# A streaming encoder step on one core: down product in groups of four feature blocks with the k-tile outermost, and the feed-forward's first weights taken up in the last residual block

## The chip, the core and the metric

The kernel runs on one core of a Trainium2 chip. A core has five engines, each with an instruction queue of its own that is worked off strictly in order: PE (TensorE, matmuls; PEld are its weight loads), DVE (VectorE), ACT (ScalarE), POOL (GpSimd) and SP (SyncE, which here issues DMA transfers). The metric is the device time of one execution in microseconds, median of several runs; lower is better.

## The reference

One inference step of a one-layer encoder for 1024 prompt tokens and 8 streams of 16 tokens, together T = 1152 tokens of width D = 1024, in float32. Only the third part is touched by the change:

```
x  = x + concat(diff_attention, short_conv) @ w_out       # token mixing
x  = x + cross_attention(x) @ w_xo                        # D x D, residual
hf = rms_norm(x, g_ffn)
u  = causal_dwconv3(hf @ w_up)                            # D -> D_FF = 2816
x  = x + (silu(u) * (hf @ w_gate)) @ w_down               # D_FF -> D
y  = rms_norm(x, g_final)
```

## The kernel before, in words

Activations lie transposed: features on the 128 partitions, tokens along the free axis. Every float32 product is made of three fp32r matmuls: each operand x is split into a high part h (a cast, on ScalarE, line 111) and a low part l = x - h (a subtraction, on VectorE or GpSimd, line 112), and h·h + h·l + l·h is summed in PSUM. So every weight block of 128x512 costs a cast and a subtraction ahead of its matmuls (`wh`, `wl`).

*Residual block with w_xo* (`residual_wino`). Eight output blocks of 128 features, each over three chunks of 384 tokens. `block` fetches and splits the weight (`wunit`), multiplies, and `evac` adds x, stores it, scales it into the halves `xa`, `xb` for the feed-forward, and adds up squares on GpSimd (`acc`). Up to here a planner orders the instructions; from the feed-forward on, the order is the one in which the code is written.

*Up and gate product* (`ffn`). One Strassen-Winograd level: for each slab s of 22 there are seven products P1 to P7 of 24 matmuls with 288 columns, `seq` lists them. Weights come as two raw tiles of 128x1024 per slab (`ffn_load`), and four sums S1 to S4 of their quarters are made on GpSimd (`ffn_sum`). The activation side has B11, B21, B22 (split at the block's end, `pair`) and the differences T1 to T4 (`tsubs` makes them, `tsplit` splits them). Before each product n, `read(n-1)` reads the PSUM sums of the last one, `split(n+3)` splits a weight three products ahead, and `at[n]` holds whatever else is due (norm ratio, convolution, gate). There are four buffers for wh and wl each, so the split for product n+4 must wait until product n is done. The gated result goes to DRAM (`gscr`).

*Down product.* The tokens are three tiles c of 512, 384 and 256 columns (`LAST`), the output eight feature blocks j, the sum over k runs over 22 k-tiles (`NFB`). A step takes one 128x512 piece of weights, split three steps ahead (`wsplit`), and mostly 12 matmuls. The list `steps` gives their order:

- tile 0, j = 0..3: k outermost, one step per k-tile, four feature blocks per step (22 steps);
- all else: one feature block j after the other, six steps of four k-tiles each (the sixth of two).

The operands of a tile (22 split pairs of gscr data) come by `qload` (DMA into one of three buffers S2, S3, S4), `qsplit` and `operands`. For tile 0 one is made per step in the first 22 steps; for tiles 1 and 2 all 22 are made during the last two feature blocks of the tile before, in 12 steps. `evac(c, j)` closes a feature block: VectorE multiplies by the norm ratio and adds the residual `ys` (fetched by `xload`), ScalarE squares and scales, GpSimd adds up the squares (in the last tile mostly VectorE). `norm1` sums over partitions on TensorE, `norm2` makes the reciprocal root and multiplies all eight blocks in one go, six on VectorE and two on GpSimd, and stores them, two of the stores being issued on ScalarE's queue.

The PSUM has four tiles `ch` of two banks each in this part.

Of the kernel before, what the change touches and what calls it, by code (L numbers as in the profile page):

```python
# [51 lines left out]
class Step:  # L52
# [122 lines left out]
    def block(self, src, xh, xl, tag, evac):  # L175

        w = self.wunit(src)
        for c in range(NCH):
# [790 lines left out]
    def residual_wino(self, wsrc, xh, xl, xsrc, dst, gi):  # L969
# [6 lines left out]
        self.Tf = [None] * 4  # L976
        for n in range(KT):
# [20 lines left out]
            self.block(wsrc[j], xh, xl, lambda c: ("mm", "tr")[(c + n) % 2], evac)  # L998
            if n % 2 == 0:
                self.B[k]["B11"] = self.pair("hl", "b", h0)  # L1000
            else:
                b11, b22, b12, b21 = xa[k][:, 0:HT], xa[k][:, HT:T], xb[k][:, 0:HT], xb[k][:, HT:T]
                self.B[k]["B21"] = self.pair("hl", "b", b21)
                self.B[k]["B22"] = self.pair("hl", "b", b22)
# [4 lines left out]
                self.tsubs = [sub(b11, b12, b11), sub(b12, b22, b12), sub(b22, b22, b11), sub(b21, b21, b22)]  # L1009
# [11 lines left out]
    def w2(self, x, view=lambda z: z):  # L1021

        m = x.shape[-1] if len(x.shape) == 2 else 512
        h, l = (self.tile("w2", t, [512], 4, F32R)[:, 0:m] for t in ("wh", "wl"))
        self.split(view(h), view(l), x)
        return h, l

    def w2_raw(self, src):
        raw = self.tile("w2", "raw", [1024], 4)[:, 0:src.shape[-1]]
# [3 lines left out]
    def ffn_load(self, s):  # L1033

        i = 4 * (s // 2) + s % 2
        r0, r1 = (self.w2_raw(self.I["w_ug"][u]) for u in (i, i + 2))
# [10 lines left out]
    def ffn(self):  # L1047
# [8 lines left out]
        first = {**reads, "P3": [("d", 1, 10)], "P6": [("b", 1, 1)], "P5": [("c", 1, 1)], "P7": [("b", 11, 10), ("c", 11, 11)]}  # L1056
        second = {**reads, "P5": [("c", 11, 10)], "P7": [("b", 11, 11)]}
        seq = [(0, "P1"), (0, "P3"), (0, "P2"), (0, "P6"), (0, "P5"), (0, "P7"), (1, "P1"), (0, "P4"),
# [4 lines left out]
        self.W, wp, ch = {}, {}, {}  # L1063
# [24 lines left out]
        def product(n):  # L1088
            s, p = seq[n]
            h, l = wp.pop(n)  # L1090
            b, c = opd[p][1], (s, "d" if (s, p) == (0, "P3") else chain[p])
# [109 lines left out]
        def ratio(t):  # L1201

            def f():
                z = self.tile("tu", "z", [T])
                v, y, r = half(z, 0), half(z, 1), half(self.r, t)
# [5 lines left out]
                nc.scalar.activation(r, y, AF.Square)  # L1211
                nc.vector.scalar_tensor_tensor(out=v, in0=v, scalar=-0.5, in1=r, op0=ALU.mult, op1=ALU.mult)
# [21 lines left out]
        put(4, tsplit("T3", (2, 3), (3,)), self.tsubs[3])  # L1234
# [3 lines left out]
        for i in range(last + 1):  # L1238
# [17 lines left out]
            else:  # L1256
                put(7, ratio(0))
                put(8, ratio(1))
# [398 lines left out]
```

## Time and profile before

| | |
|---|---|
| median of 3 runs | 1733.08 us (1730.76 to 1733.68) |
| the profiled execution: its time, its span | 1735.62 us, 1733.8 us |
| PE busy, share of the span | 1669.3 us, 96% |
| DVE, ACT, POOL busy | 60%, 39%, 24% |
| granted TensorE clock, mean | 0.980 |
| L111 casts of weights, ACT, 128x512 | 607 ns mean |
| L112 low parts of weights, DVE, 128x512 | 702 ns mean |
| L112 low parts of weights, POOL, 128x512 | 1326 ns mean |

A row of a timeline reads: start, duration, engine, line, operation, output <- input, shapes, count, and in brackets the idle time of the engine before it with what ended it. PE's busy share says little by itself, since matmuls are pipelined and a slowed clock also counts as busy; the distance of starts tells the rate. A wait is put down to the instruction that came last.

### The profile page before, as it was taken

The numbers are of one execution on the slowest core, as the hardware profiler recorded it, in microseconds if no ns is written. First come the engines' busy times: TensorE is split into PE (matmuls) and PEld (weight loads), VectorE is DVE, ScalarE is ACT, GpSimd is POOL, SyncE is SP. The second block draws the span as 40 slices with busy tenths as digits, with TensorE's granted clock in tenths as the row PEclk, the third lists the DMA queues.
The fourth block names the chain that finished last, engine by engine and source line by source line (L and its number), as shares of the span: only waits on it lengthen the run. The fifth ranks groups of instructions, "written<-read, shape, count | busy, mean of one in ns | idle before, by whom it ended". The sixth has DMA issues, their size and how long they took to land.

```text
span 1733.8 us, 28155 instructions
## 1 busy us (share of the span) xinstructions
PE 1669.3 (96%) x10930; PEld 1579.6 (91%) x10930; DVE 1045.0 (60%) x1707; ACT 678.1 (39%) x1382; POOL 413.9 (24%) x443
## 2 busy tenths in 40 slices
PE   8999989999999999999989999999999999979887
PEld 7999879989899999989988999999999998869787
DVE  8757545777733343376658766666666664444465
ACT  7222543655513332263335433333333354433443
POOL 3223322111113321101335333233223212120100
PEclk9999999999999999999989999999999999999989
DMA  5756877434264434532431222221222265455553
GB/s 197 252 189 208 283 255 197 152 110 128 92 260 142 133 110 183 182 147 85 136 121 38 78 78 78 78 71 64 74 77 78 77 193 173 147 172 173 160 185 123
DMA packets 111366, 246.09 MB, mean 142 GB/s; under 512 B 18176, under 2 KB 63104, under 8 KB 111232
## 3 DMA queue, kind: packets, MB, share of 16 engines
q1 hardware_dynamic: 110368, 243.11, 43.1%
q8 instruction: 86, 1.41, 0.3%
q10 hardware_dynamic: 864, 1.18, 0.2%
q14 instruction: 48, 0.39, 0.1%
HBM read 186.86 MB, written 57.39 MB: 141 GB/s over the span
## 4 chain that ended last, share of the span: by engine, by line
PE 80%; DVE 6%; DMA 5%; ACT 4%; issue 2%; POOL 1%; SPq 0%; DVEq 0%; ACTq 0%; POOLq 0%
PE ch L1102 27%; PE ch L1381 11%; PE mm L148 8%; PE mm L150 8%; PE mm L149 8%; PE tr L148 3%; PE tr L149 3%; PE tr L150 3%; DMA S<-gscr 2%; PE tr L653 2%; DMA ys<-x 1%; PE sc L614 1%; PE tr L640 1%; ACT wh L111 1%; DVE ys L1364 1%
## 5 line engine op out<-in xcount | busy, mean ns | idle before, releaser
L111 ACT CAST wh<-raw 128x512 fp32r<-128x512 f32 x338 | 201.5, 607 | 346.5 <-PE ch L1102 99.9
L112 DVE TENSOR_TENSOR wl<-raw,wh 128x512 fp32r<-128x512 f32 (+1 forms) x284 | 196.6, 702 | 226.2 <-ACT wh L111 225.3
L1102 PE MATMUL ch<-t,wh 128*128 128x288 f32 x1408 | 284.9, 297 | 3.9 <-DVE xb L1111 3.7
L1102 PEld LDWEIGHTS ch<-t,wh 128*128 128x128 f32 x1408 | 227.5, 189 | 4.6 <-issue 3.9
L1102 PE MATMUL ch<-b,wh 128*128 128x288 f32 x1056 | 216.8, 300 | 5.5 <-ACT wh L111 5.5
L1102 PE MATMUL ch<-t,wl 128*128 128x288 f32 x704 | 208.0, 296 | 0.0
L112 POOL TENSOR_TENSOR wl<-raw,wh 128x512 fp32r<-128x512 f32 x54 | 71.5, 1326 | 450.8 <-ACT wh L111 412.6
L1102 PEld LDWEIGHTS ch<-b,wh 128*128 128x128 f32 x1056 | 172.6, 191 | 6.2 <-ACT wh L111 6.0
L148 PE MATMUL mm<-xh,wh 128*128 128x384 f32 x496 | 169.7, 342 | 0.9 <-DVE t L822 0.9
L150 PE MATMUL mm<-xh,wl 128*128 128x384 f32 x496 | 167.9, 338 | 0.0
L149 PE MATMUL mm<-xl,wh 128*128 128x384 f32 x496 | 167.7, 338 | 0.0
L1102 PE MATMUL ch<-b,wl 128*128 128x288 f32 x528 | 157.4, 298 | 0.5 <-DVE wl L112 0.5
L1381 PE MATMUL ch<-t,wh 128*128 128x512 f32 (+2 forms) x544 | 139.5, 343 | 6.5 <-ACT wh L111 6.3
L1102 PEld LDWEIGHTS ch<-t,wl 128*128 128x128 f32 x704 | 133.5, 190 | 0.0
L1381 PEld LDWEIGHTS ch<-t,wh 128*128 128x128 f32 x544 | 97.0, 192 | 15.4 <-ACT wh L111 7.9
L1381 PE MATMUL ch<-b,wh 128*128 128x256 f32 (+2 forms) x384 | 95.8, 341 | 13.0 <-ACT wh L111 13.0
L1102 PEld LDWEIGHTS ch<-b,wl 128*128 128x128 f32 x528 | 101.1, 191 | 1.0 <-DVE wl L112 1.0
L1381 PE MATMUL ch<-t,wl 128*128 128x512 f32 (+2 forms) x272 | 94.0, 346 | 2.8 <-DVE wl L112 2.5
L148 PEld LDWEIGHTS mm<-xh,wh 128*128 128x128 f32 x496 | 93.3, 188 | 3.7 <-issue 1.6
L149 PEld LDWEIGHTS mm<-xl,wh 128*128 128x128 f32 x496 | 93.4, 188 | 0.4
L150 PEld LDWEIGHTS mm<-xh,wl 128*128 128x128 f32 x496 | 93.4, 188 | 0.1
L1045 POOL TENSOR_TENSOR S<-raw,raw 128x512 f32<-128x512 f32 x44 | 72.1, 1640 | 68.1 <-DVE wl L112 63.6
(374 smaller groups left out, 3730.2 us busy)
## 6 DMA issues: line engine op xcount, KB each, us to landing
raw<-in_w_dn SPq DMA_DIRECT2D x51, 512.0 KB, 4.4
raw<-in_w_ug SPq DMA_DIRECT2D x44, 512.0 KB, 4.5
gscr<-xb SPq DMA_DIRECT2D x22, 576.0 KB, 3.2
kv<-in_kc SPq DMA_DIRECT2D x16, 512.0 KB, 5.6
kv<-in_vc SPq DMA_DIRECT2D x16, 512.0 KB, 6.3
qd<-qscr SPq DMA_DIRECT2D x64, 128.0 KB, 3.8
kv<-in_km SPq DMA_DIRECT2D x16, 512.0 KB, 6.0
kv<-in_vm SPq DMA_DIRECT2D x16, 512.0 KB, 5.6
```

Of the source, the lines that this page charges most:

```text
L111: self.nc.scalar.copy(out=h, in_=x)
L112: (eng or self.nc.vector).tensor_tensor(out=l, in0=x, in1=fl(h), op=ALU.subtract)
L148: self.nc.tensor.matmul(out, lhsT=ah, rhs=bh, start=i == 0, stop=False)
L149: self.nc.tensor.matmul(out, lhsT=ah, rhs=bl, start=False, stop=False)
L150: self.nc.tensor.matmul(out, lhsT=al, rhs=bh, start=False, stop=i == n - 1)
L614: nc.tensor.matmul(sc[:, a:b], lhsT=qd[:, m, hl, (i % 2) * P:(i % 2 + 1) * P], rhs=ks[m][:, a:b], start=hl == 0, stop=hl == 1)
L640: nc.tensor.transpose(tr[:, j * P:(j + 1) * P], a[:, kt * P:(kt + 1) * P], self.ident)
L653: nc.tensor.matmul(av[:, qs], lhsT=at[kt // 4][:, kt % 4, qs], rhs=vt[:, kt], start=kt == 0, stop=kt == n - 1)
L1045: self.nc.gpsimd.tensor_tensor(out=w[o], in0=w[x], in1=w[y], op=op)
L1102: nc.tensor.matmul(o, lhsT=w[:, ks], rhs=y[:, ts], start=start and k == 0 and i == 0, stop=k == 3 and i == 2, skip_group_check=True)
L1364: eng.tensor_tensor(out=ys[c, j], in0=ys[c, j], in1=r, op=ALU.mult)
L1381: nc.tensor.matmul(ch[c, j], lhsT=p[:, w], rhs=y, start=k == 0 and e == 0, stop=k == NFB - 1 and e == 2)
```

## The change

1. In the last residual block, right after its own weight is fetched, the first slab's two raw tiles are loaded and its four sums made (`first`, called by `block` through the new argument `then`). The pool `weights` therefore stays open, and the feed-forward's raw tiles and split weights use its buffers together with a smaller pool `w2`: again four raw tiles and four pairs in all.
2. The first slab's products run in the order P1, P2, P3 and go to three PSUM tiles of their own (chains a, d, e); the splits of the last B21 and B22 come after the first two weight splits; the norm ratio of each half is made in two pieces, `ratio1` and `ratio2`, one place apart.
3. The down product runs with k outermost in groups of four feature blocks for tile 0, tile 1 and the first half of tile 2 (110 steps); only the last four feature blocks of tile 2 keep the old form (24 steps). Weights for the groups come from an array laid out so that a load is one contiguous block.
4. The operands of the next tile are made one per step during the second group of a tile, with six buffers in place of three; their low parts on VectorE only (for tile 0 every third stays on GpSimd).
5. A group's four `evac` stand in the first four steps of the next group, its residual loads in the last four steps of its own. `norm1` comes after step 7, `norm2` at step 9 of the next tile's first group, and the final multiplies (`norm3`) one per step in steps 10 to 17, for tiles 0 and 1 all on VectorE and stored by SP.

The core of the diff:

```diff
+        def first():
+            self.ffn_load(0)
+            for d in range(4):
+                self.ffn_sum(0, d)
...
-            self.block(wsrc[j], xh, xl, lambda c: ("mm", "tr")[(c + n) % 2], evac)
+            self.block(wsrc[j], xh, xl, lambda c: ("mm", "tr")[(c + n) % 2], evac, first if n == KT - 1 else None)
...
-        seq = [(0, "P1"), (0, "P3"), (0, "P2"), (0, "P6"), (0, "P5"), (0, "P7"), (1, "P1"), (0, "P4"),
+        seq = [(0, "P1"), (0, "P2"), (0, "P3"), (0, "P6"), (0, "P5"), (0, "P7"), (1, "P1"), (0, "P4"),
...
-                put(7, ratio(0))
-                put(8, ratio(1))
-                put(9, rho(0, 0), rho(0, 10))
+                put(7, ratio1(0))
+                put(8, ratio2(0), ratio1(1))
+                put(9, rho(0, 0), rho(0, 10), ratio2(1))
...
-        steps = [(0, range(4), (k,)) for k in range(NFB)]
-        steps += [(c, (j,), range(4 * u, min(4 * u + 4, NFB)))
-                  for c in range(len(LAST)) for j in range(0 if c else 4, KT) for u in range(6)]
+        steps = [(c, range(4 * g, 4 * g + 4), (k,)) for c in range(3) for g in range(2) for k in range(NFB) if (c, g) != (2, 1)]
+        NG = len(steps)
+        steps += [(2, (j,), range(4 * u, min(4 * u + 4, NFB))) for j in range(4, KT) for u in range(6)]
...
-            graw[q] = self.tile("ws", ("S2", "S3", "S4")[q % 3], [512])[:, 0:b - a]
+            e = q % 6 if c else q % 3
+            graw[q] = self.tile("ws" if e < 3 else "t8", ("S2", "S3", "S4")[e % 3], [512])[:, 0:b - a]
...
-            self.split(h, l, x, nc.gpsimd if q % 3 == 0 else None)
+            self.split(h, l, x, nc.gpsimd if q < NFB and q % 3 == 0 else None)
...
         for i, (c, js, ks) in enumerate(steps):
+            g, k = js[0] // 4, ks[0]
             wsplit(i + 3)
...
+            if len(js) > 1:
+                if k < 4 and i >= NFB:
+                    evac(*((c, k) if g else (c - 1, 4 + k)))
+                if g == 0 and c and k == 9:
+                    norm2(c - 1)
+                if g == 0 and c and 9 < k < 18:
+                    norm3(c - 1, k - 10)
+                if 18 <= k:
+                    xload(c, 4 * g + k - 18)
+                if g and c < 2:
+                    operands(NFB * (c + 1) + k + 1, 6)
...
+            if len(js) == 1 and js[0] == 4 and ks[0] < 16:
+                evac(c, k // 4)
             step(i)
...
-            j = js[0]
-            if c < 2 and j >= 6:
-                operands(NFB * (c + 1) + (ks[0] // 4 + 1 if j == 6 else min(10 + ks[0], NFB)))
+            if g == 0 and c and len(js) > 1 and k == 7:
+                norm1(c - 1)
```

How the change moves instructions, at three places. First GpSimd at the end of the residual block (`acc` are the sums of squares of the last chunks, `S` and `raw` the first and second slab's weight sums, `t` the low parts of T3 and T4). Before:

```order
L225 TENSOR_TENSOR acc_8210<-acc_8210,sq_9078 128x384
L225 TENSOR_TENSOR acc_8210<-acc_8210,sq_9112 128x384
L225 TENSOR_TENSOR acc_8210<-acc_8210,sq_9145 128x384
L1045 TENSOR_TENSOR S_1661_9178<-raw_9174,raw_9176 128x512
L1045 TENSOR_TENSOR raw_9176<-raw_9176 128x512
L1045 TENSOR_TENSOR S_1662_9181<-raw_9176,raw_9174 128x512
L1045 TENSOR_TENSOR S_1663_9183<-raw_9174,S_1662_9181 128x512
```

The same place in the changed kernel:

```order
L1059 TENSOR_TENSOR S_1648_9052<-raw_9048,raw_9050 128x512
L1059 TENSOR_TENSOR raw_9050<-raw_9050 128x512
L1059 TENSOR_TENSOR S_1649_9055<-raw_9050,raw_9048 128x512
L1059 TENSOR_TENSOR S_1650_9057<-raw_9048,S_1649_9055 128x512
L227 TENSOR_TENSOR acc_8210<-acc_8210,sq_9089 128x384
L227 TENSOR_TENSOR acc_8210<-acc_8210,sq_9123 128x384
L227 TENSOR_TENSOR acc_8210<-acc_8210,sq_9156 128x384
```

The four sums of the first slab moved ahead of the last block's three sums of squares.

Second, VectorE at the same place (`xc` the last evacuated chunk, `b` low parts of B21 and B22 of the last k-tile, `wl` low parts of the first weights). Before:

```order
L988 TENSOR_TENSOR xc_9140<-tr_9115,xc_9140 128x384
L993 SCALAR_TENSOR_TENSOR xa_8922<-xc_9140,c_6_79,c_9_84 128x384
L112 TENSOR_TENSOR b_9153<-xa_8922,b_9152 128x576
L112 TENSOR_TENSOR wl_9190<-raw_9174,wh_9189 128x512
L112 TENSOR_TENSOR wl_9194<-S_1663_9183,wh_9193 128x512
L112 TENSOR_TENSOR wl_9198<-raw_9174,wh_9197 128x512
```

Now:

```order
L998 TENSOR_TENSOR xc_9151<-tr_9126,xc_9151 128x384
L112 TENSOR_TENSOR wl_9185<-raw_9048,wh_9184 128x512
L1003 SCALAR_TENSOR_TENSOR xa_8922<-xc_9151,c_6_79,c_9_84 128x384
L112 TENSOR_TENSOR b_9189<-xb_8923,b_9188 128x576
L112 TENSOR_TENSOR b_9193<-xa_8922,b_9192 128x576
L112 TENSOR_TENSOR wl_9197<-S_1650_9057,wh_9196 128x512
```

P1's low part is no longer here (it stands two chunks earlier), P2's stands right behind the last PSUM read, and the split of B21 now comes after it.

Third, ScalarE at the handover from token tile 0 to tile 1 (`t`, `gx`, `b` are operand casts for tile 1, `wh` weight casts, `sq` and `ys` the square and the scale of an evacuation). Before:

```order
L111 CAST t_15631<-S_2558_15597 128x384
L111 CAST t_15637<-S_2561_15603 128x384
L111 CAST t_15643<-S_2564_15609 128x384
L111 CAST t_15649<-S_2571_15635 128x384
L111 CAST wh_15655<-raw_15437 128x512
L111 CAST gx_15671<-S_2574_15641 128x384
L111 CAST gx_15677<-S_2577_15647 128x384
L111 CAST gx_15683<-S_2580_15653 128x384
L111 CAST gx_15689<-S_2585_15675 128x384
L111 CAST wh_15695<-raw_15437 128x512
```

Now:

```order
L111 CAST b_15653<-S_2547_15513 128x384
L111 CAST wh_15671<-raw_15507 128x512
L111 CAST b_15677<-S_2552_15535 128x384
L111 CAST wh_15695<-raw_15507 128x512
L226 ACTIVATE sq_15704<-ys_15601 128x512
L1366 ACTIVATE ys_15601<-ys_15601,c_6_79 128x512
L111 CAST wh_15722<-raw_15553 128x512
L226 ACTIVATE sq_15729<-ys_15625 128x512
L1366 ACTIVATE ys_15625<-ys_15625,c_6_79 128x512
L111 CAST wh_15745<-raw_15553 128x512
```

Operand casts stood four between two weight casts; now one stands between two, and after the handover a square and a scale stand between every two weight casts, four times over.

More of the change, by code (lines that the diff above doesn't have):

```diff
@@ L173, in finish, with block @@
             self.todo.pop(0)()
-    def block(self, src, xh, xl, tag, evac):
+    def block(self, src, xh, xl, tag, evac, then=None):
         w = self.wunit(src)
+        if then:
+            then()
         for c in range(NCH):
@@ L1018, in pair, with w2, w2_raw @@
         return h, l
[L1021 to L1025, printed above, removed]
+    def w2(self, x):
+        m = x.shape[-1]
+        self.wn += 1
+        h, l = (self.tile("w2" if self.wn % 4 == 2 else "weights", t, [512], 1 if self.wn % 4 == 2 else 3, F32R)[:, 0:m]
+                for t in ("wh", "wl"))
+        self.split(h, l, x)
         return h, l
-    def w2_raw(self, src):
-        raw = self.tile("w2", "raw", [1024], 4)[:, 0:src.shape[-1]]
+    def w2_raw(self, src, odd):
+        raw = self.tile("w2" if odd else "weights", "raw", [1024], 2)[:, 0:src.shape[-1]]
         self.nc.sync.dma_start(out=raw, in_=src)
@@ L1318, in qsplit, with operands @@
             x = graw.pop(q)
-            e = q % 28
-            pool, tag, bufs = ("tb", "t", 24) if e < 12 else ("t8", "gx", 8) if e < 16 else ("hl", "b", 24)
-            h, l = (self.tile(pool, tag, [512 if pool == "t8" else HT], bufs, F32R)[:, 0:x.shape[-1]] for _ in range(2))
-            self.split(h, l, x, nc.gpsimd if q % 3 == 0 else None)
+            pool, tag = ("tb", "t") if q % 24 < 12 else ("hl", "b")
+            h, l = (self.tile(pool, tag, [HT], 24, F32R)[:, 0:x.shape[-1]] for _ in range(2))
+            self.split(h, l, x, nc.gpsimd if q < NFB and q % 3 == 0 else None)
             gx[divmod(q, NFB)] = h, l
-        def operands(upto):
+        def operands(upto, lead=3):
             while done[0] < min(upto, 3 * NFB):
@@ L1353, in norm1 @@
             a, b = LAST[c]
-            ch[c] = self.bank("ch")[:, 0:b - a]
+            ch[c] = ch[c, 4]
             for i, z in enumerate(sq[c]):
@@ L1370, in step @@
             h, l = wp.pop(N + i)
-            for j in js:
+            for e, j in enumerate(js):
                 if (c, j) not in ch:
@@ L1377, in step @@
                 for x, k in enumerate(ks):
-                    w = slice((j if len(js) > 1 else x) * P, (j if len(js) > 1 else x) * P + P)
+                    w = slice((e + x) * P, (e + x + 1) * P)
                     gh, gl = gx[c, k]
-                    for e, (p, y) in enumerate(((h, gh), (h, gl), (l, gh))):
-                        nc.tensor.matmul(ch[c, j], lhsT=p[:, w], rhs=y, start=k == 0 and e == 0, stop=k == NFB - 1 and e == 2)
-        self.ffn_load(0)
-        sums(0, 0, 1, 2, 3)()
+                    for m, (p, y) in enumerate(((h, gh), (h, gl), (l, gh))):
+                        nc.tensor.matmul(ch[c, j], lhsT=p[:, w], rhs=y, start=k == 0 and m == 0, stop=k == NFB - 1 and m == 2)
         new_u(0)()
-        for n in range(3):
-            split(n)
-        for f in self.tsubs[:3]:
+        split(0)
+        split(1)
+        for f in self.tsubs[:2]:
+            f()
+        split(2)
+        for f in self.tsubs[2:5]:
             f()
```

106 lines of the change are left out of this document (52 added, 54 removed).

## The prediction

> **What bounds the kernel now.** I read the stages first, then what TensorE waits for in them, then what stands ahead of those releasers on their own engines. All times are of the one profiled execution: its span is 1733.8 us and its own time 1735.6, that is 1.8 more, and 2.5 above the median of the three runs (1733.1).
>
> The stage table (columns: stage, length, busy us of PE, PEld, DVE, ACT, POOL, granted clock, DMA share, GB/s):
> ```profile
> 892.97:946.20 53.23, 43.05 (x272) 41.03 (x273) 38.62 (x50) 25.87 (x44) 23.38 (x18) 0.89 0.17 54
> 946.20:1405.40 459.20, 459.20 (x3431) 459.20 (x3432) 321.75 (x417) 165.74 (x251) 140.81 (x186) 0.99 0.24 78
> 1519.50:1562.60 43.10, 32.13 (x149) 27.06 (x147) 22.93 (x36) 18.53 (x36) 8.95 (x7) 0.92 0.55 174
> 1618.80:1668.90 50.10, 37.55 (x217) 34.52 (x215) 26.32 (x46) 22.10 (x48) 9.67 (x10) 0.86 0.55 173
> 1668.90:1722.90 54.00, 53.36 (x413) 52.54 (x414) 28.98 (x54) 23.40 (x46) 0.00 (x0) 0.94 0.51 159
> ```
> The last residual block ends at 892.97, the down product runs from 1405.4 to 1722.9. TensorE is the bound nearly everywhere: 459.2 of 459.2 us in the body of the feed-forward. In the part that the change touches three stretches leave it idle: the first 53 us of the feed-forward and the two handovers between token tiles of the down product (43.1 and 50.1 us).
>
> How far from TensorE's own limit the down product is, I get from the distance of starts at full clock, three matmuls each:
> ```profile
> 1514.06 0.62 PE L1381 MATMUL ch<-t,wh 128*128 128x512 f32 x2
> 1514.74 0.62 PE L1381 MATMUL ch<-t,wh 128*128 128x512 f32 x2
> 1578.32 0.51 PE L1381 MATMUL ch<-b,wh 128*128 128x384 f32 x2
> 1578.84 0.51 PE L1381 MATMUL ch<-b,wh 128*128 128x384 f32 x2
> 1690.08 0.40 PE L1381 MATMUL ch<-b,wh 128*128 128x256 f32 x2
> 1690.44 0.40 PE L1381 MATMUL ch<-b,wh 128*128 128x256 f32 x2
> ```
> 0.68, 0.52 and 0.36 us per three: 0.227, 0.173 and 0.120 each. Every tile takes 8 x 22 x 3 = 528 of them, so the stage costs TensorE 528 x 0.52 = 274.6 us, against 317.5 taken. 42.9 us are lost: some 2 of them to norm sums on TensorE, which stay. Who is waited for, and what holds ScalarE up (columns: us in total, times, longest):
> ```profile
> PE ch L1381 <- ACT wh L111: 21.3, 10, 6.3
> ACT t L111 <- DMA S<-gscr: 17.5, 10, 3.7
> ACT wh L111 <- DMA out_yT<-ys: 5.5, 1, 5.5
> ACT b L111 <- DMA S<-gscr: 5.3, 4, 3.5
> ACT sq L224 <- DVE ys L1344: 35.6, 17, 3.1
> ```
> TensorE waits for the next weight's high part, a ScalarE cast. That cast isn't slow: it stands in ScalarE's queue behind operand casts that wait for their DMA (17.5 + 5.3 us), because all 22 operands of the next tile are asked for in the last 12 steps with three buffers, and once behind the burst of final multiplies and its two stores on ScalarE's queue (5.5). 21.3 us are direct waits; most of the remaining 20 is reduced clock behind them, as the 0.92, 0.86 and 0.94 of the stages say.
>
> The start of the feed-forward, same columns:
> ```profile
> PE ch L1102 <- ACT wh L111: 5.5, 2, 2.9
> PE ch L1102 <- DVE xb L1111: 3.7, 1, 3.7
> DVE wl L112 <- ACT wh L111: 8.9, 3, 7.7
> DVE z L1212 <- ACT c L1211: 4.4, 2, 2.2
> 895.50 0.53 PE L1102 MATMUL ch<-b,wh 128*128 128x288 f32 x2 [2.53 <-ACT wh L111]
> 898.16 1.28 POOL L1045 TENSOR_TENSOR S<-raw,raw 128x512 f32<-128x512 f32 x1 [2.90 <-DMA raw<-in_w_ug]
> 903.51 0.62 ACT L111 CAST wh<-S 128x512 fp32r<-128x512 f32 x1 [8.06 <-POOL u L1177]
> 904.18 0.85 PE L1102 MATMUL ch<-b,wh 128*128 128x288 f32 x2 [2.93 <-ACT wh L111]
> 906.03 0.68 PE L1102 MATMUL ch<-b,wh 128*128 128x288 f32 x2
> 906.75 0.68 PE L1102 MATMUL ch<-b,wh 128*128 128x288 f32 x2
> 910.33 0.43 PE L1102 MATMUL ch<-b,wh 128*128 128x288 f32 x2
> 925.85 1.54 DVE L1111 TENSOR_TENSOR u<-ch,u 128x576 f32<-128x576 f32 x2
> ```
> P1 waits for a weight load issued after the block, P3 for four GpSimd sums of that load; meanwhile ScalarE and VectorE stand still (8.06 and 7.7 us). After each gap the matmuls run at half speed: 0.24 us each (three from 906.03 to 906.75) against 459.2/3431 = 0.134 in the body, until 910.3, where two take 0.43 instead of 0.68. Of the stage's 272 matmuls eight are the norm sum's; 264 of 0.134 make 35.3 us, so some 36 to 37 of the 53.2 are work. A third gap, 3.7 us, is a PSUM read that VectorE does late.
>
> **The change part by part.** *Loads and sums in the last residual block.* Two 512 KB loads on SP's queue, four sums on POOL, one weight split on ScalarE and VectorE. The first load finds a free buffer; the second waits until the last block's own weight is split, and on SP the block's x loads stand behind it. The sums take 4 x 1.28 = 5.1 us, behind the last block's matmuls:
> ```profile
> 879.17 0.68 DVE L112 TENSOR_TENSOR wl<-raw,wh 128x512 fp32r<-128x512 f32 x1
> 880.05 0.32 SPq L987 DMA_DIRECT2D xc<-x  x1
> 867.00:892.97 25.97, 25.97 (x150) 25.65 (x148) 15.14 (x22) 6.20 (x11) 7.64 (x7) 1.00 0.36 111
> ```
> That split ends at 879.85, when the block's first x load goes out anyway (880.05); the second weight load follows it at once and holds nobody. POOL is busy 7.6 of 26 us there, and TensorE never waits. The squares' sums queued behind them are needed only by the sixth product. If that cover is gone, about 5 us fall back onto the block's end. I cost it at nothing.
>
> *P1, P2, P3 as separate sums.* One more PSUM read on VectorE (0.77, half of the row at 925.85), one ScalarE copy less. P1 no longer waits for anything but its bank; P2 and P3 have their weights. Splitting the ratio in two takes away the 4.4 us in which VectorE stood behind ScalarE, or most of it. What is late next is VectorE: it was busy 38.6 of 53.2 us; plus 0.8, less two weight splits done before (2 x 0.7), it needs 38.0. So the gain is at most 53.2 - 38.0 = 15.2, and at least the 2.9 of P3's wait. VectorE's T3 and T4 splits come just in time for P7 and late for P4 (in its order some 3 us late), and one half-speed spell as from 904.2 to 910.1 costs 5.9 x (1 - 0.134/0.24) = 2.6. I take 15.2 - 3 - 2.6 = 9.6, nearer the upper end since VectorE is the row that is left.
>
> *Down product, k outermost.* The matmuls stay 1584 of the same shapes; weight units go from 142 to 134, the loads stay as large. Operands of the next tile are now split one per step over 22 steps, with six buffers, so a load has six steps (12 us or more) instead of three: the 17.5 + 5.3 us go. The two stores leave ScalarE and the eight final multiplies are spread over eight steps: the 5.5 go.
>
> What is new: at each of five handovers, four evacuations stand in four successive steps, each between two weight splits. One such evacuation in the old kernel:
> ```profile
> 1539.51 0.69 DVE L112 TENSOR_TENSOR wl<-raw,wh 128x512 fp32r<-128x512 f32 x1
> 1540.11 0.68 DVE L1343 TENSOR_TENSOR sq<-ch,c 128x512 f32<-128x512 f32 x1
> 1540.83 0.69 DVE L1344 TENSOR_TENSOR ys<-sq,ys 128x512 f32<-128x512 f32 x1
> 1541.62 0.63 ACT L224 ACTIVATE sq<-ys 128x512 f32<-128x512 f32 x1 [2.23 <-DVE ys L1344]
> 1542.28 0.72 ACT L1350 ACTIVATE ys<-ys,c 128x512 f32<-128x512 f32 x1
> 1542.91 1.95 ACT L111 CAST wh<-raw 128x512 fp32r<-128x512 f32 x4
> 1543.55 2.23 DVE L112 TENSOR_TENSOR wl<-raw,wh 128x512 fp32r<-128x512 f32 x4 [2.02 <-ACT wh L111]
> ```
> It is a circle: ScalarE's square waits for VectorE's add, the next cast stands behind square and scale, VectorE's next split waits for that cast. From the split at 1539.51 to the next at 1543.55 a turn takes 4.0 us, with TensorE's end and the hops of a full turn (0.1 to 0.2) some 4.2, for 512 columns. For a narrower tile (last number before the bar: mean ns of one):
> ```profile
> L1343 DVE TENSOR_TENSOR sq<-ch,c 128x384 f32<-128x384 f32 x8 | 4.4, 551 | 0.0
> L1350 ACT ACTIVATE ys<-ys,c 128x384 f32<-128x384 f32 x8 | 4.9, 618 | 0.3
> ```
> each of four operations (multiply, add, square, scale) takes 0.10 to 0.13 less for 128 columns fewer: 3.7 for 384 and, the same step on, 3.2 for 256. Where an operand's cast stands in it too, 0.5 or 0.4 more. A step of TensorE takes 12 matmuls: 2.72, 2.08, 1.44 us. Four weight pairs give a lead of three steps: the split of the fourth step on is ready 1.4 + 4 turns after the handover's begin and wanted after 7 steps. Stall = 1.4 + 4 x turn - 7 x step: 1.2 within tile 0 (turn 4.7), 3.6 from tile 0 to 1 (4.2), 3.2 within tile 1 (4.1), 6.1 from tile 1 to 2 (3.7), 4.1 within tile 2 (3.2): 18. Bounds: 0, if the circle is looser than I read it, and 4 x (turn - step) summed, 40, if the lead is worth nothing. I take 18, since the circle's rows are of this very code.
>
> Reduced clock behind these stalls: between 0 and five spells of 2.6 = 13; pieces of 1 to 2.3 us are nearer to nothing than the gaps of 2.5 and more, so 4. The Trainium skill, TensorE: Matmul & The Clock Gate, section HAM oscillation, says that only idle gaps over about 3.4 us halve the clock; the rows at 895.50 and 906.03 differ, with half speed after 2.5 to 2.9 us. By that page's figure, an estimate, the clock term would be 0 and the time 4 us shorter.
>
> The last tile's end is as before: one sum, the norm, eight multiplies, 10.9 us.
>
> The sum: down product 274.6 + 2 + 18 + 4 = 298.6, 18.9 less; start 9.6 less. Span 1733.8 - 28.5 = 1705.3; the execution 1707.1; the median 1704.6, so 1705.
>
> **The rivals.** *The evacuations hide.* No stall and no reduced clock in the down product: 40.9 less, with the start 1733.1 - 50.5 = 1683. For it: in the stretch 1668.90 to 1722.90 single evacuations leave TensorE busy 53.36 of 54. Against: those stand six steps apart.
> *The start gains nothing.* VectorE's backlog eats it: about 1714.
> *The stalls trade one for one.* The lead is worth nothing, 40 us come back: 1723 to 1733. Against it: four weight pairs did cover single turns.
> *Slower: the clock stays low.* The stalls of 1 to 2.3 us, 1.4 us of work apart, hold TensorE at half speed beyond the handover. Each us so spent costs half a us; to undo 28.5 it must last 57 us, as long as a whole group of tile 0. At 80 us the time is about 1745. Against it: after 904 it was over in 6 us.
>
> **How the numbers follow.** My forecast 0.62, with its own range 1694 to 1717; hidden evacuations 0.22; no gain at the start 0.08; one for one 0.05; low clock 0.03. The range 1680 to 1719 leaves out some 0.1 of the hidden case (below 1680, towards 1677, if the start reaches its bound as well), the trade and the low clock: 0.18 in all. Differences under 0.2% (3.5 us) can't be told from none here. Faster: 0.62 + 0.22 + 0.08 + 0.03 of the trade's 0.05 = 0.95; same 0.02; slower 0.03.
>
> **What would show it.** Right: no wait of ScalarE for gscr loads; P1 starting within 1 us of the block's end and no wait for GpSimd sums; TensorE's waits in the down product only in steps 5 to 7 of each handover, longest from tile 1 to 2; ScalarE's square still waiting about 2 us for VectorE. Wrong: waits of TensorE spread over whole groups, a granted clock under 0.9 over tens of us, or stalls in the last residual block.

## The result, and the profile after

| | us, median | runs |
|---|---|---|
| before, beside it on the same chip | 1733.04 | 1730.76 to 1733.68, 4 |
| changed | 1702.95 | 1700.45 to 1704.68, 4 |

The ratio is 0.9828 [0.9811, 0.9845]: 30.1 us faster. Runs on other chips further down put the kernel before at 1734.5 to 1735.9, so there only ratios and differences against the kernel before of the same row are compared.

The page of the changed kernel; the profiled execution took 1700.45 us, 2.5 below its median:
```profile
span 1698.7 us, 28128 instructions
...
PE 1651.9 (97%) x10930; PEld 1566.5 (92%) x10930; DVE 1047.9 (62%) x1718; ACT 675.9 (40%) x1373; POOL 395.6 (23%) x425
```
The span is 35.1 us shorter than in the profile before, 5 more than the medians, since the profile before was taken 2.5 us above its median and this one 2.5 below. 3.4 of these lie ahead of the feed-forward (889.6 in place of 892.97), nearly all in code that was not touched: the matmuls of the last residual block take as long as before. The profiles of the runs below put this point anywhere from 889.3 to 894, so I leave these 3.4 us out. In stages (columns: stretch, length, then busy time and number of instructions of PE, PEld, DVE, ACT, POOL, the granted clock, the DMA share, GB/s):
```profile
889.60:950.00 60.40, 50.89 (x356) 49.43 (x355) 52.14 (x67) 31.62 (x51) 25.98 (x24) 0.94 0.18 57
...
1516.00:1562.00 46.00, 44.37 (x248) 42.61 (x247) 25.72 (x40) 19.17 (x32) 5.14 (x4) 1.00 0.54 172
...
1609.00:1642.00 33.00, 29.11 (x219) 27.61 (x218) 20.56 (x37) 16.75 (x31) 4.02 (x4) 1.00 0.50 153
1642.00:1688.20 46.20, 44.50 (x341) 43.52 (x340) 26.05 (x50) 20.89 (x41) 0.00 (x0) 0.93 0.52 169
```
The feed-forward up to the end of the up and gate products runs from 889.6 to 1395.9, 506.3 us in place of 512.4: **6.1 us** gained. The down product runs from 1396.0 to the last norm sum at 1687.8, 291.8 in place of 317.1 by the same measure (start of its first matmul to start of the last tile's norm sum): **25.3 us** gained. In the down product TensorE now stands still only in short pieces. What it waits for from the feed-forward on (columns: us in total, times, longest):
```profile
PE ch L1399 <- ACT wh L111: 7.1, 7, 1.4
PE ch L1118 <- DVE xb L1127: 5.3, 1, 5.3
PE ch L1118 <- DVE u L1127: 3.0, 1, 3.0
PE ch L1399 <- DVE wl L112: 0.9, 4, 0.2
PE ch L1118 <- DVE t L112: 0.8, 1, 0.8
```
L1118 is the up and gate product, L1399 the down product. Before, the down product waited 21.3 us for `wh`, in waits of up to 6.3. And ScalarE's waits inside the down product, the two longest:
```profile
ACT wh L111 <- PE ch L1399: 104.4, 81, 2.3
ACT sq L226 <- DVE ys L1360: 36.0, 19, 2.2
```
The first row is a cast that waits for a free buffer, which is what a cast does when it is ahead of its time. In the whole list no row names gscr any more, nor a wait of 5.5 us for a store. One row still names a store (`ACT wh L111 <- DMA out_yT<-ys`, 2.9 us in two waits), but these two are 1.46 us each, as long as their neighbours' waits for a free buffer. So the transfers no longer hold ScalarE up. What is left is its wait for VectorE's add. The turn at the handover from tile 1 to tile 2, in order of time:
```profile
1617.11 0.69 DVE L112 TENSOR_TENSOR wl<-raw,wh 128x512 fp32r<-128x512 f32 x1 [1.81 <-ACT wh L111]
1617.71 0.55 DVE L1359 TENSOR_TENSOR sq<-ch,c 128x384 f32<-128x384 f32 x1
1618.30 0.56 DVE L1360 TENSOR_TENSOR ys<-sq,ys 128x384 f32<-128x384 f32 x1
1618.95 0.53 ACT L226 ACTIVATE sq<-ys 128x384 f32<-128x384 f32 x1 [1.88 <-DVE ys L1360]
1619.51 0.62 ACT L1366 ACTIVATE ys<-ys,c 128x384 f32<-128x384 f32 x1
1620.03 0.60 ACT L111 CAST wh<-raw 128x512 fp32r<-128x512 f32 x1
1620.67 0.69 DVE L112 TENSOR_TENSOR wl<-raw,wh 128x512 fp32r<-128x512 f32 x1 [1.81 <-ACT wh L111]
```
Each engine idles 1.8 us in every turn because it waits for the other: one turn, 3.56 us, for 1.75 us of ScalarE's own work and 1.8 of VectorE's. TensorE's step is 1.44 us here.

### The profile page after: what moved, and what is told of

Same layout as the page of the kernel before. It is cut to its first block, busy times and chain, and to the rows that moved or that the text cites. A ratio compares the mean times of both kernels' runs of the same rounds, so it can differ in the third digit from the quotient of the medians.

```text
span 1698.7 us, 28128 instructions
## 1 busy us (share of the span) xinstructions
PE 1651.9 (97%) x10930; PEld 1566.5 (92%) x10930; DVE 1047.9 (62%) x1718; ACT 675.9 (40%) x1373; POOL 395.6 (23%) x425
## 5 line engine op out<-in xcount | busy, mean ns | idle before, releaser
L111 ACT CAST wh<-raw 128x512 fp32r<-128x512 f32 x330 | 202.0, 617 | 352.0 <-PE ch L1399 104.4
L1118 PE MATMUL ch<-t,wh 128*128 128x288 f32 x1408 | 284.4, 297 | 9.2 <-DVE xb L1127 5.3
L1118 PEld LDWEIGHTS ch<-t,wh 128*128 128x128 f32 x1408 | 227.1, 189 | 10.0 <-issue 8.8
L1118 PE MATMUL ch<-b,wh 128*128 128x288 f32 x1056 | 212.9, 296 | 0.0
L1118 PE MATMUL ch<-t,wl 128*128 128x288 f32 x704 | 207.9, 295 | 0.0
L1118 PEld LDWEIGHTS ch<-b,wh 128*128 128x128 f32 x1056 | 169.4, 188 | 0.2
L1118 PE MATMUL ch<-b,wl 128*128 128x288 f32 x528 | 155.3, 294 | 0.0
L1399 PE MATMUL ch<-t,wh 128*128 128x512 f32 (+2 forms) x576 | 146.4, 341 | 6.0 <-ACT wh L111 5.9
L1118 PEld LDWEIGHTS ch<-t,wl 128*128 128x128 f32 x704 | 133.2, 189 | 0.0
L1399 PE MATMUL ch<-b,wh 128*128 128x512 f32 (+2 forms) x480 | 119.6, 337 | 1.2 <-ACT wh L111 1.2
L1399 PEld LDWEIGHTS ch<-t,wh 128*128 128x128 f32 x576 | 102.2, 193 | 16.1 <-ACT wh L111 7.9
L1399 PE MATMUL ch<-t,wl 128*128 128x512 f32 (+2 forms) x288 | 98.5, 342 | 1.0 <-DVE wl L112 0.7
L1118 PEld LDWEIGHTS ch<-b,wl 128*128 128x128 f32 x528 | 99.4, 188 | 0.0
L1399 PEld LDWEIGHTS ch<-b,wh 128*128 128x128 f32 x480 | 84.3, 190 | 7.8 <-ACT wh L111 1.4
```

Source lines behind the costliest of these rows:

```text
L111: self.nc.scalar.copy(out=h, in_=x)
L1118: nc.tensor.matmul(o, lhsT=w[:, ks], rhs=y[:, ts], start=start and k == 0 and i == 0, stop=k == 3 and i == 2, skip_group_check=True)
L1399: nc.tensor.matmul(ch[c, j], lhsT=p[:, w], rhs=y, start=k == 0 and m == 0, stop=k == NFB - 1 and m == 2)
```

## The experiments

All are timed against the kernel before. "Down" is the down product of that run's profile, first matmul to the last tile's norm sum (317.1 before, 291.8 changed); "body" is the feed-forward from its first matmul up to the down product's (510.1 before, 506.5 changed).

| run | median us | before there | ratio | body | down |
|---|---|---|---|---|---|
| start only | 1728.19 | 1735.91 | 0.9957 [0.9945, 0.9970] | 506.6 | 314.6 |
| down product only | 1708.38 | 1735.91 | 0.9843 [0.9830, 0.9856] | 509.6 | 292.1 |
| evacuations spaced | 1694.20 | 1735.91 | 0.9764 [0.9748, 0.9780] | 506.7 | 283.2 |
| ratio later | 1698.76 | 1735.91 | 0.9786 [0.9773, 0.9800] | 502.9 | 291.8 |
| square later | 1688.32 | 1734.54 | 0.9735 [0.9717, 0.9754] | 506.2 | 276.4 |
| square and ratio later | 1682.97 | 1734.54 | 0.9705 [0.9687, 0.9724] | 501.6 | 277.4 |
| operands bunched | 1704.22 | 1734.54 | 0.9828 [0.9809, 0.9847] | 506.5 | 293.1 |
| changed kernel again | 1702.48 | 1734.54 | 0.9817 [0.9799, 0.9835] | 506.2 | 291.8 |
| bunched, three buffers | 1719.32 | 1735.18 | 0.9910 [0.9896, 0.9923] | 506.6 | 312.3 |
| old operands | 1721.39 | 1735.18 | 0.9923 [0.9908, 0.9937] | 506.2 | 311.0 |
| spread, three buffers | 1702.74 | 1735.18 | 0.9812 [0.9797, 0.9827] | 507.3 | 291.6 |
| before, no burst | 1726.28 | 1735.18 | 0.9949 [0.9935, 0.9962] | 510.0 | 312.5 |

### Which part carries the gain

**Start only**: parts 1 and 2 of the change, with `steps`, `wload`, `operands`, `norm2` and the weight layout of the kernel before.

> The start of the feed-forward as in the changed kernel (weights and sums in the last block, the new order of products, the ratio in two parts), the down product as in the kernel before. Theory: the two parts of the change stand for themselves, and the start is worth what the two profiles show, 512.4 - 506.3 = 6.1 us, so 1727 us (1725 to 1729), with the down product at 317 to 318 us. Rival 1: most of those 6.1 us belong to the down product's side (the weight buffers and their rotation), so 1731 to 1733. Rival 2: the start is worth the 9.6 us of the prediction, and the profile of the changed kernel lost some of it by chance, so 1723 to 1724.

7.7 us faster. The body is that of the changed kernel, as the theory has it. The down product, whose order is that of before, reads 314.6 in place of 317.1; only the rotation of the weight buffers differs there, so either it is worth up to 2.5 us or two profiles of one order differ by that much. One profile each does not settle it, though five profiles of the new order lie closer together (291.6 to 292.1).

**Down product only**: parts 3 to 5, with the start of before.

> The down product as in the changed kernel, the start of the feed-forward as before. Theory: gain 317.5 - 292.0 = 25.5 us by the profiles, so 1707 to 1709 us. Rival: the down product's gain needs the other rotation of the weight buffers (three of wh and wl in one pool and one in the other), so under 20 us of gain, over 1713.

27.5 us faster; the down product reads 292.1, as in the whole change. The rival with the buffers falls: it does as well without them.

**The changed kernel again**, beside the later runs:

> The changed kernel itself once more, beside these on the same chip, since the start alone (ratio 0.9957) and the down product alone (0.9843) add up to 0.0200 and the whole measured 0.0172. If the parts simply add, it reads 0.980 to 0.982 here and the first reading was low; if they share something, 0.9828 again.

The two parts by themselves add up to 2.00% with some 0.2 of uncertainty, the whole reads 1.72 and 1.83%. So the parts add, as far as these runs can tell. The down product carries four fifths.

### What stalls TensorE at the handovers now

**Evacuations spaced**: every second step in place of four steps running.
```diff
-                if k < 4 and i >= NFB:
-                    evac(*((c, k) if g else (c - 1, 4 + k)))
-                if g == 0 and c and k == 9:
+                if k < 8 and k % 2 == 0 and i >= NFB:
+                    evac(*((c, k // 2) if g else (c - 1, 4 + k // 2)))
+                if g == 0 and c and k == 11:
```
(with `norm3`, `norm1` and the last tile's evacuations moved likewise)

> The changed kernel with the four evacuations of a group in every second step (k = 0, 2, 4, 6; the norm's sum, its square root and the eight products two steps later) instead of in four steps running. Theory (the circle cast, evacuation, square, scale, next cast sets the pace of a step that has an evacuation): a turn of 4.05 us plus one more cast of 0.60 has two steps of 2.72 us, one of 3.56 plus 0.60 has two of 2.08 or of 1.60. By 1.4 + 4 x (turn + 0.6) - 11 x step no handover has a stall but that from tile 1 to tile 2 (1.4 + 16.6 - 17.7 = 0.4 us) and the one inside tile 2 (about 1); the half-speed spell behind the last one goes too. Down product 292.0 -> 277 to 280 us, time 1688 to 1692 us. Rival 1 (the weights or operands are late at those places, and the evacuations only stand in the line): 1701 to 1705, waits for wh as before. Rival 2 (the wait moves to the norm's steps, since the second group's first tile needs the bank that the norm's sum holds): 1696 to 1700, with waits of PE at the start of the groups.

41.7 us under the kernel before of the same runs, where the changed kernel is 30.1 to 32.1 under its own: some 10 to 12 us gained, 8.6 in the down product's profile. The time lies between theory and rival 2; of rival 2's mark, waits at the norm's steps, there is one of 0.5 us. TensorE's longest wait in its down product:
```profile
PE ch L1399 <- ACT wh L111: 2.2, 3, 0.8
```
7.1 us of waits for `wh` have become 2.2, all of them in tile 2, at 1620.8 (0.55), 1656.9 and 1659.9; the first three handovers, up to that inside tile 1, are clean. The miss is in tile 2: I had put its step at 1.60 us, it is 1.44. A turn with a second cast measured 4.16 us (1620.80 to 1624.96, from split to split), and 1.4 + 4 x 4.16 - 11 x 1.44 = 2.2 in place of 0.4. Spacing helps, but it does not open the circle.

**Square later**: the same four steps running; only the order in ScalarE's queue changes. `evac` keeps VectorE's multiply and add; a new `evac2` has the square, its sum and the scale, and is called one step later (the last tile's evacuations likewise, in lines not shown here).
```diff
+                if 0 < k < 5 and i >= NFB:
+                    evac2(*((c, k - 1) if g else (c - 1, 3 + k)))
                 if k < 4 and i >= NFB:
                     evac(*((c, k) if g else (c - 1, 4 + k)))
```


> The changed kernel with the four evacuations in the same four steps running, but ScalarE's square and scale of each one step later, so that in ScalarE's queue they stand behind the next weight cast. Nothing is taken out or spread. Theory (circle): the cast no longer waits for VectorE's multiply and add of the same step, so that a turn is the larger of ScalarE's own work (0.60 + 0.53 + 0.62 = 1.8 us) and VectorE's (0.69 + 0.55 + 0.56, less overlap, 1.7), and 4 turns of 1.8 lie below 7 steps of 1.44: no stall at any of the five handovers, the norm's sums apart, and no half speed after them. Down product 292.0 -> 276 to 278 us; 13.5 to 16 us faster than the changed kernel, a ratio to the kernel before of 0.973 to 0.976. Rival 1 (the work of four evacuations in four steps is too much for ScalarE and VectorE, and only spreading them helps): under 4 us. Rival 2 (weights arrive late there): no difference.

14.2 us under the changed kernel of the same runs, inside the theory's 13.5 to 16; the down product takes 276.4 in place of 291.8. From the feed-forward on, all of TensorE's waits are now these:
```profile
PE ch L1118 <- DVE xb L1127: 5.3, 1, 5.3
PE ch L1118 <- DVE u L1127: 3.0, 1, 3.0
PE ch L1378 <- ACT sum L1368: 0.6, 1, 0.6
```
No wait of the down product (L1404 in this kernel) is left, the norm's sum at the very end apart. The same handover from tile 1 to 2, ScalarE's rows:
```profile
1612.37 0.53 ACT L226 ACTIVATE sq<-ys 128x384 f32<-128x384 f32 x1 [0.40 <-DVE ys L1360]
...
1613.45 0.60 ACT L111 CAST wh<-raw 128x512 fp32r<-128x512 f32 x1
1614.50 0.53 ACT L226 ACTIVATE sq<-ys 128x384 f32<-128x384 f32 x1 [0.45 <-DVE ys L1360]
```
From square to square 2.13 us in place of 3.56, and 0.45 us of idling in place of 1.88. This is not the 1.8 that I expected, since VectorE's add takes 1.02 us here in place of 0.56 (see the last section), but 1.4 + 4 x 2.13 - 7 x 1.44 = -0.2 still leaves no stall. Same work, same steps, nothing spread: the circle alone held TensorE up, and it cost 15.4 us with the half speed behind it. Rivals 1 and 2 fall.

### What the old handover lost

**Operands bunched**: the changed kernel with the next tile's operands at the old pace, up to four per step.
```diff
-                    operands(NFB * (c + 1) + k + 1, 6)
+                    operands(NFB * (c + 1) + (max(0, k - 9) if k < 16 else min(4 * k - 54, NFB)), 6)
```


> The changed kernel with the next tile's operands no longer one per step of the second group: one per step in steps 10 to 15, and four per step in steps 16 to 19, as the kernel before did in its last unit; six buffers as in the changed kernel, no split on GpSimd. Theory: a load is issued only when the split before it in its buffer is done, so four splits in a step wait for loads issued in the step before, ScalarE stands behind them (3 us each in the kernel before), and the waits for gscr loads are back at two places, two stalls of 3 to 6 us and the half speed behind them: 6 to 14 us slower than the changed kernel, ratio to before 0.986 to 0.991. Rival 1 (the loss before was the evacuation burst and the strided weight loads, not the operands): within 2 us of the changed kernel. Rival 2 (six buffers cover it): within 2 us too, with no wait of ScalarE for these loads.

1.7 us slower than the changed kernel of the same runs. The intervals of the two ratios overlap, but each of its four times (1703.1 and more) lies above each of the other's (1702.9 and less), so a small loss is likely. My theory of the transfers falls in this form; the time is the rivals', but rival 2's mark, no wait for these loads, is not there. ScalarE does wait for the loads again, in this stretch:
```profile
ACT b L111 <- DMA S<-gscr: 7.2, 3, 3.6
...
ACT t L111 <- DMA S<-gscr: 4.4, 2, 2.9
```
but 11.6 us of it in five waits, and the lead of the weights covers them: TensorE's waits for `wh` are 6.9 us (7.1 in the changed kernel).

**Bunched, three buffers**: the same with `e = q % 3` in `qload` and a lead of three loads.

> As e5 (operands bunched, four per step in steps 16 to 19), and with three buffers as in the kernel before instead of six. Theory, mended after e5: not the bunching but bunching with three buffers stopped ScalarE. Three loads go out together and land 3 to 3.6 us later; 16 operands then take some 5.3 rounds of 4 us = 21 us in place of 4 steps (10.9 or 8.3 us); the lead of three steps (8.2 or 6.2) hides part, and the evacuations that follow find no lead. Two stalls of 4 to 7 us: 8 to 15 us slower than the changed kernel, ratio to the kernel before 0.986 to 0.991, ScalarE waiting 15 to 25 us for gscr loads. Rival: with k outermost a tile needs one operand per step, so lateness is paid once at most and the evacuation stalls swallow it: within 3 us of the changed kernel, and the loss of the kernel before came from its order (24 evacuations and 22 operands all due at once).

16.6 us slower than "spread, three buffers" of the same runs, above the theory's 8 to 15; ScalarE's 29.7 us of waits for these loads also lie above its 15 to 25. ScalarE's waits for these loads and TensorE's for the casts:
```profile
ACT b L111 <- DMA S<-gscr: 14.9, 8, 3.5
ACT t L111 <- DMA S<-gscr: 14.8, 9, 3.7
```
```profile
PE ch L1399 <- ACT wh L111: 16.7, 11, 4.2
```
Where it happens, in ScalarE's rows at the handover from tile 0 to 1:
```profile
1512.56 0.62 ACT L111 CAST wh<-raw 128x512 fp32r<-128x512 f32 x1
1513.08 0.92 ACT L111 CAST b<-S 128x384 fp32r<-128x384 f32 x2
1515.62 0.52 ACT L111 CAST b<-S 128x384 fp32r<-128x384 f32 x1 [1.62 <-DMA S<-gscr]
1519.65 0.51 ACT L111 CAST b<-S 128x384 fp32r<-128x384 f32 x1 [3.52 <-DMA S<-gscr]
1520.07 0.61 ACT L111 CAST wh<-raw 128x512 fp32r<-128x512 f32 x1
```
Between two weight casts stand four operand casts and two waits for loads: 7.5 us for a step of 2.72. TensorE then stands still for 4.2 us, until 1520.74.

**Old operands**: as above, and `nc.gpsimd if q % 3 == 0` in `qsplit`, as before for all tiles.

> As e10, and every third operand's low part on GpSimd as in the kernel before: the whole old preparation of operands under the new order of the product. Theory: GpSimd's split of 1.3 us and more holds its buffer longer, so 1 to 4 us slower than e10. Rival: GpSimd takes work off VectorE, which the evacuations wait for: as e10 or up to 2 us faster.

1721.39 against 1719.32, intervals overlapping. The 2.1 us would fit the theory, but the runs of the two scatter over the same times (1718.4 to 1726.3 and 1718.7 to 1721.2), so they do not tell it from the rival's "as e10".

**Spread, three buffers**: one operand per step as in the changed kernel, three buffers as before.

> The changed kernel (one operand per step over 22 steps) with three buffers instead of six. Theory: a load has three steps (8.2 us for tile 1's operands, 6.2 for tile 2's) and lands after 3 to 4: nothing waits, within 1.5 us of the changed kernel, ratio 0.981 to 0.983; the six buffers then are worth nothing by themselves. Rival: loads queue behind the weights on the same queue, and a few ScalarE waits for gscr come back: 2 to 5 us slower.

1702.74: the time of the changed kernel. In one point the expectation was wrong, ScalarE does wait for the loads (its fourth longest wait in that stretch), but in pieces of about 1 us that nobody feels:
```profile
ACT t L111 <- DMA S<-gscr: 9.4, 10, 2.3
```
So neither the six buffers nor the even pace is worth anything alone; one of them is needed, and the lack of both costs 17 to 19 us.

**Before, no burst**: the kernel before with its eight final multiplies of tiles 0 and 1 one per weight unit, all stores by SP.
```diff
-            for j in (0, 6, 1, 2, 7, 3, 4, 5):
-                eng, q = (nc.vector, nc.sync) if j < 6 else (nc.gpsimd, nc.scalar)
-                eng.tensor_tensor(out=ys[c, j], in0=ys[c, j], in1=r, op=ALU.mult)
-                q.dma_start(out=self.O["yT"][j, :, a:b], in_=ys[c, j])
+            sq[c] = r
...
+            if c and (js[0], ks[0]) in spread:
+                norm3(c - 1, spread.index((js[0], ks[0])))
```


> The kernel before with one edit: the eight final multiplies of tiles 0 and 1 one per weight unit instead of eight running, none on GpSimd, their stores all on SyncE's queue instead of two on ScalarE's. Theory: the two stalls at 1558 and 1667 us (2.3 + 1.5 + 0.3 and 3.2 + 1.1 lost, 8.4 us) go and nothing comes in their place: 7 to 9 us faster, ratio 0.995 to 0.996. Rival: the stall is the norm's square root chain, not the burst, and stays: under 3 us.

8.9 us faster by the times, inside the theory's range, though its profile, taken in the slowest of its six executions, shows only 4.6 us in the down product (312.5). Both stalls, at 1558 and at 1667, are gone. In tile 2 new ones have come, which TensorE's rows show:
```profile
1666.77 0.50 PE L1382 MATMUL ch<-t,wh 128*128 128x256 f32 x2 [1.01 <-ACT wh L111]
...
1677.75 0.50 PE L1382 MATMUL ch<-t,wh 128*128 128x256 f32 x2 [2.33 <-ACT wh L111]
```
Ahead of the second, VectorE's add had waited 3.79 us, until 1675.78, for its residual load. SP issued that load at 1669.93, behind stores of the later multiplies in its queue, and it landed 5.8 us after. Whether the queue delayed it or the `ys` buffers, of which the kernel before has 11 (the changed one 12), no run separates. So "nothing comes in their place" was half right.

The two sizes, 16.6 and 8.9 us, add up to 25.5, about what the down product gained. That is no account of it, since the changed kernel pays for the circle (15.4 us, "square later") and its gain is what is left after that. The kernel before took 317.1 - 276.4 = 40.7 us more than "square later". By the distances of its matmuls' starts 11.5 and 14.4 of these lie where the operands of tiles 1 and 2 arrive, 5.3 and 7.1 behind the two bursts, the rest in small pieces; 40.7 - 15.4 = 25.3. So the operands cost up to 26 us in the old order and 17 to 19 in the new one. What else adds to the 26, no run separates.

### The start of the feed-forward

**Ratio later**: the second half's Ln, Exp and Square one step later (`power`), its two products another step later, each behind that step's read.
```diff
-                put(9, rho(0, 0), rho(0, 10), ratio2(1))
-                put(10, rho(0, 11), rho(0, 1), streams(0, 1), tap0(0, 1))
+                put(9, power(1), rho(0, 0), rho(0, 10))
+                put(10, ratio2(1), rho(0, 11), rho(0, 1), streams(0, 1), tap0(0, 1))
```
In the changed kernel VectorE's rows ahead of the 5.3 us wait read:
```profile
932.89 0.69 DVE L112 TENSOR_TENSOR wl<-S,wh 128x512 fp32r<-128x512 f32 x1 [3.23 <-ACT wh L111]
933.50 1.42 DVE L1132 TENSOR_TENSOR u<-u,c 128x576 f32<-128x576 f32 x2
934.83 0.75 DVE L1234 SCALAR_TENSOR_TENSOR z<-z,c 128x576 f32<-128x576 f32 x1
935.62 0.76 DVE L1235 SCALAR_TENSOR_TENSOR c<-z 128x576 f32<-128x576 f32 x1
936.29 0.75 DVE L1127 TENSOR_TENSOR xb<-ch,xb 128x576 f32<-128x576 f32 x1
```
The last row is the read for which TensorE, whose last matmul ended at 931.84, has been waiting. VectorE had idled 3.23 us for a weight cast, which stood on ScalarE behind the root's three steps and a copy, and then did four products first.

> The changed kernel with the second half's ratio cut once more: its Ln, Exp and Square on ScalarE one step later (behind that step's read and weight cast), its two products on VectorE another step later (behind that step's read). Theory: the 5.5 us in which PE waits at 931.55 for the read of the product before are queueing: the read stands on VectorE behind a weight split whose cast stands on ScalarE behind Ln, Exp and Square (2.1 us), and behind four products (2.9 us). With them behind the reads the 5.5 us go, and the half speed up to 941 with them (0.11 to 0.13 us lost per matmul, some 2.7 us): 1695 to 1698 us. Rival: VectorE is full over these steps as a whole (the taps and the later products move back by 3 us), so that a wait of 3 to 6 us stands some 6 us later: 1700 to 1704.

37.2 us under the kernel before of the same runs, 5 to 7 us more than the changed kernel's 30.1 to 32.1; the body's profile is 3.6 us shorter. So the wait was queueing, as the theory has it. What TensorE waits for up to the body's end:
```profile
PE ch L1118 <- DVE u L1127: 3.0, 1, 3.0
PE ch L1118 <- ACT xb L1165: 0.8, 1, 0.8
...
PE ch L1118 <- DVE xb L1127: 0.3, 1, 0.3
```
The 5.3 us are 0.3 now. 0.8 us came back later, as the rival has it, in much smaller size. A half-speed spell from 910 to 917, which the first profile of the changed kernel does not have, takes some 1.4 us off the profile's gain: "square and ratio later", whose start is the same and whose profile has no such spell, has a body of 501.6 us in place of 502.9 (last section).

**Square and ratio later**: both edits.

> The square and scale one step later, and the ratio's second half behind the reads (e7). The two lie 500 us apart; the gains should add: 14.5 + 5.5 = 20 us under the changed kernel, ratio to the kernel before 0.970 to 0.973. Rival: e7's gain came from the earlier stages of its run (the stages ahead of the feed-forward differ by up to 5 us from run to run), then it is that of e8 alone within 2 us.

1682.97 us, ratio 0.9705 [0.9687, 0.9724]: 19.5 us under the changed kernel of the same runs, 51.6 under the kernel before. 14.2 of it come from the square, 5.3 from the ratio. It is the fastest of all, and beats both kernels.

## Why the prediction was right, and where its steps were off

The forecast was 1705, measured were 1702.95. The mechanisms were right in the main, but that the sum came so close is partly luck: two of its terms were off in opposite directions, the down product by 6.4 us (18.9 forecast, 25.3 measured) and the start by 3.5 (9.6 and 6.1).

*The circle.* Shown, as a mechanism: changing only the place of square and scale took 14.2 us off the time and every wait out of the down product. The marks named in advance are there: ScalarE's square waiting up to 2.2 us for VectorE, and TensorE's waits in the down product only in steps 5 to 7 of a group, the longest run from tile 1 to 2. Its rows there, without the 0.2 us pieces:
```profile
1620.69 0.50 PE L1399 MATMUL ch<-t,wh 128*128 128x256 f32 x2 [0.47 <-ACT wh L111]
...
1624.24 0.51 PE L1399 MATMUL ch<-t,wh 128*128 128x256 f32 x2 [1.38 <-ACT wh L111]
...
1627.81 0.51 PE L1399 MATMUL ch<-t,wh 128*128 128x256 f32 x2 [1.37 <-ACT wh L111]
```

*Its size: the terms "handover stalls 18" and "reduced clock 4" were too large.* Together with the half speed they measured 15.4 (291.8 less 276.4), not 22. By handover, from the distances of the matmuls' starts, lost time against predicted stall: 0 for 1.2, 2.7 for 3.6, 2.0 for 3.2, 5.5 for 6.1, and within tile 2 some 2.7 for 4.1 plus 2.6 of half speed (some 28 matmuls 0.213 us apart in place of 0.120). The turns were read too long, 4.05 and 3.56 us in place of 4.2 and 3.7; with these the formula gives 1.4 + 4 x 4.05 - 7 x 2.08 = 3.0 and 1.4 + 4 x 3.56 - 7 x 1.44 = 5.6 for tile 0 to 1 and 1 to 2. The step "with the hops of a full turn 0.1 to 0.2" that rounded the row's 4.04 up failed: these hops lay in the row already. The 1.4, for which the prediction shows no row, was too long as well: from a group's start to the first matmul of step 7, less four turns, are 0.5 to 0.7 us at the three handovers from tile 0 to 1, within tile 1 and from tile 1 to 2. Half speed came once, not five times in part.

*The 274.6 and the two norm sums* held: without stalls the down product took 276.4.

*Operands and burst.* The prediction gave each its wait on ScalarE (22.8 and 5.5 us) and let both go. It passed over two rows of the same list of the kernel before, a third one of operands and the cast behind GpSimd's share of the second burst:
```profile
ACT wh L111 <- POOL ys L1364: 4.4, 1, 4.4
...
ACT gx L111 <- DMA S<-gscr: 3.0, 2, 2.2
```
Both went too. Right in effect, but it named "one per step over 22 steps, with six buffers" as one cause. The runs show that either alone would do.

*The start: 9.6 predicted, 6.1 measured.* The failed step is "splitting the ratio in two takes away the 4.4 us in which VectorE stood behind ScalarE, or most of it". The wait changed its place: VectorE no longer stands behind the root itself, but behind a weight split whose cast stands behind the root, 3.23 us, and the PSUM read behind both. TensorE lost 5.3 us there, which were not in the sum. It is the first matmul of the twelfth product, the same at which the kernel before had its third gap, 3.7 us at 946.20: that gap did not go, it grew. Taken out ("ratio later", "square and ratio later") the 5.3 us gave some 5. The 3 us for VectorE's lateness had the right size, but came earlier than P4: 3.0 at P7, for a PSUM read that stood on VectorE behind a split of T3, and 0.8 within P7, for the next such split. The one half-speed spell (937 to 941) was right. P1 started without a gap, and no wait for the first slab's GpSimd sums was left, as predicted; ScalarE still waited 3.6 us once, at 916.45, for one of the second slab's (4.0 before), and no wait of TensorE names it.

*The rivals.* That the evacuations hide was wrong for this kernel, yet its price of 40.9 us for the down product is what the order of "square later" gets (40.7: 276.4 in place of 317.1). None of the others showed.

## What to carry to other kernels

When two in-order engines hand work to each other both ways within a step, a turn costs the sum of both (3.56 us here, for 1.75 and 1.8 us of work); issue the half that waits one step later, behind the work that others wait for, and a turn comes near the larger of the two (2.13 us here). It is worth trying before work is spread or removed: here it gave 15.4 us in the down product for a few moved lines, and spacing gave 8.6. The burst of loads here needed buffers or an even pace, not both; which of the two a change really lives on is seen only by taking them away one at a time.

## What the runs showed of the hardware

*Half speed does not follow from the length of a gap alone.* Windows (the granted clock is the third number from the end) of the changed kernel:
```profile
911.50:917.00 5.50, 5.50 (x38) 5.29 (x39) 5.19 (x6) 1.23 (x3) 3.47 (x2) 1.00 0.20 67
...
937.10:941.00 3.90, 3.81 (x16) 3.84 (x17) 3.22 (x5) 2.65 (x4) 2.63 (x5) 0.50 0.07 9
```
```profile
1660.00:1668.00 8.00, 7.55 (x34) 6.82 (x35) 5.72 (x12) 4.21 (x9) 0.00 (x0) 0.58 0.36 111
1621.00:1629.00 8.00, 4.58 (x30) 3.57 (x29) 4.32 (x9) 4.54 (x9) 1.99 (x2) 1.00 0.24 66
```
and of "ratio later", the same place in the program as the first of these:
```profile
911.30:917.00 5.70, 5.67 (x20) 5.10 (x21) 5.31 (x7) 1.40 (x3) 3.45 (x2) 0.51 0.20 67
```
Both kernels wait 3.03 us shortly before, for the same read, and then 0.8 and 0.6 us; one goes on at full clock, the other at half. Eleven of the profiles have this wait of 3.03 us: over the 5.5 us from its end the granted clock is 1.00 in six of them and 0.50 to 0.69 in five, and the changed kernel itself stands on both sides (1.00, and 0.69 when it ran again). The gap of 1.25 us at 1659.95 brought half speed, the gaps of 0.5, 1.4 and 1.4 us from 1620.69 to 1627.81 none. The Trainium skill, TensorE: Matmul & The Clock Gate, section HAM oscillation, which lets only gaps over about 3.4 us halve the clock, does not cover the case after 1.25 us, nor the five after 3.03. What else enters, perhaps how busy TensorE was over a stretch with edges of its own, these runs do not tell.

*VectorE beside GpSimd.* In "square later" VectorE's add takes 1.02 us while GpSimd's sum of squares runs. In the changed kernel, where the two do not meet, it takes 0.56 us for the same shape, and so does the first add of this handover (1611.71), ahead of any sum. VectorE's row and GpSimd's:
```profile
1615.51 1.02 DVE L1360 TENSOR_TENSOR ys<-sq,ys 128x384 f32<-128x384 f32 x1
```
```profile
1615.10 1.01 POOL L227 TENSOR_TENSOR sum<-sum,sq 128x384 f32<-128x384 f32 x1 [1.11 <-ACT sq L226]
```
The add ends about 0.4 us after GpSimd does, in each of three turns. With it VectorE's work in a turn is 2.24 us, less a little overlap, in place of 1.8, and the turn is 2.13 us.
